# Paged decoding inside a hybrid decoder step: ScalarE's order at the softmax, and the rotated keys put last

## The chip, the core and the metric

One core of a Trainium2 chip runs the whole program. The metric is the device time of one execution in microseconds. Three executions of the kernel before gave 3480.07, 3480.68 and 3483.55 us.

## What is computed

The reference is one inference step of a trunk of two layers. Each layer projects its input once and feeds three groups of heads (a state-space mixer, latent attention, a gated delta rule); their outputs are joined, projected and normalised. It does this for a prompt of 1024 positions and for 8 sequences that decode 4 positions each. The change lies in the latent attention of these 8 sequences, which looks at 8192 cached positions per sequence:

```python
def attend(blk):
    ql, qr, qp = blk
    s = (jnp.einsum('bthr,bsr->bhts', ql, kv_lat)
         + jnp.einsum('bthd,bsd->bhts', qr, k_rope)).astype(jnp.float32) * MLA_SCALE
    s = jnp.where(k_pos[None, :] <= qp[:, None], s, -jnp.inf)
    p = jax.nn.softmax(s, axis=-1).astype(kv_lat.dtype)
    return jnp.einsum('bhts,bsr->bthr', p, kv_lat)
```

A cached position has a latent row of 256 numbers (`kv_lat`, which serves as key and as value) and a rotated key of 32 numbers (`k_rope`). With 8 heads and 4 new positions, each sequence has 32 queries. The cache is paged, so its rows are gathered by index.

## The kernel before, in words

Phase 2 of a layer (`phase2`, line 1422) holds the attention and the output projection. Two generators are woven into each other there by `weave_decode` (line 434): the decoding (`decode_units`, line 1691) and the attention of the prompt (`mla_prompt`, line 1488). The decoding yields a number, an amount of TensorE time; `weave_decode` then takes steps of the prompt's generator until they have paid that amount by the builder's clock, each step at 0.45 or more, and carries what is left over or overspent to the next yield. So the numbers in the yields say how much prompt work stands at which place of the decoding. Inside this weaving the order of the instructions of TensorE and of VectorE is the order of the program text; the orders of ScalarE, of GpSimd and of the DMA queues are planned by the framework's scheduler, which takes what is ready in its own plan, and of several ready instructions the one with the highest priority, by default the earliest in the text. `high_priority()` raises the priority of the instructions in its block. On the chip each engine follows its fixed order and waits for semaphores.

The decoding of a layer has 32 units, 8 sequences times 4 parts of 2048 positions. A unit does the following (names of tiles as the profile has them):

- `load` (line 1682) gathers the rows of a part with three indirect DMAs from GpSimd's queue (line 1680): two for latent rows into one of three buffers (dec_v<-cache_kv_latent), one for rotated keys into a ring of three (dec<-cache_k_rope). It is called at the end of a unit for the part three units on; the latents' buffer is free when the weighted values of this unit are done, the rotated keys' slot when VectorE has turned the keys in it.
- `turn` (line 1703, instruction at line 1704) turns half of the latent rows on VectorE in squares of 32, so that they can serve as keys (dec_k<-dec_v). Line 1773 (line 1759 for the first unit) does the same for the rotated keys (dec<-dec, into rT).
- `products` (line 1706) multiplies queries and keys on TensorE into the tile ps_dS: parts 0 to 3 are the first half of the latents' 256 numbers, 4 to 7 the second half, part 8 the rotated keys. Each part is 8 multiplications in tiles of 32 x 32, two records each in the profile, so 16 records a part and 144 a unit. There is one such tile.
- `softmax` (line 1714): VectorE takes the maximum over ps_dS (line 1717) and brings it into the form in which ScalarE needs it (lines 1720 to 1726); ScalarE takes the exponential and its sum (line 159, dec<-ps_dS,dec).
- `turned` (line 1734): TensorE turns the weights (ps_aT<-c,dec, 32 records), and ScalarE copies them out (line 1740, dec<-ps_aT).
- `weighted` (line 1743): TensorE multiplies weights and latent rows (ps_dV<-dec_v,dec, 32 records); `total` (line 1750) adds the result to the sequence's sum on VectorE (line 156, dec<-dec,dec,ps_dV).

The turning of the next unit's keys stands inside the unit: rotated keys and first half before `turned`, second half before `weighted`. After the third unit `decode_new` (line 1646) handles the new positions; its first step takes the bank of ps_dV.

The prompt's steps in between are products ps_aS, their maximum (line 1558, VectorE), the exponential (line 159, c<-ps_aS,c), a scaling of the weights by their sum (line 1575, ScalarE, after line 1571 on VectorE), the turning of the weights (ps_aT at line 150, copied out at line 1515 by ScalarE) and the weighted values ps_aO.

Line 180 is the helper that records every multiplication, line 150 every full transpose, lines 153, 156 and 159 those of VectorE, GpSimd and ScalarE.

Of the kernel before, what the change touches and what calls it, by code (L numbers as in the profile page):

```python
# [16 lines left out]
AF = mybir.ActivationFunctionType  # L17
# [7 lines left out]
SCALE = 96.0 ** -0.5  # L25
# [102 lines left out]
class Builder:  # L128
# [1562 lines left out]
    def decode_units(self, d):  # L1691

        nc, G, T, q5, q8, O = self.nc, d["G"], d["T"], d["q5"], d["q8"], d["O"]
        D = d["D"].rest()
        RP, RT, rT = Ring(D(1024)), Ring(D(1024)), D(512)
        rT4 = rT.rearrange("p (n c k) -> p n c k", n=8, c=2)
        H = [slice(0, 64), slice(64, 128)]  # L1700
        tmp = D(8)

        def turn(V, r):
            nc.vector.transpose(T[r].rearrange("p j s k -> p j (s k)"), V[:, :, r * 128:r * 128 + 128])  # L1704

        def products(b, sc, parts):
            for s in parts:
                for i, p in enumerate(G):
                    for c in range(2):
                        k = rT4[p, :, c] if s == 8 else T[s // 4].rearrange("p (n c) s k -> p n c s k", c=2)[p, :, c, s % 4]  # L1710
                        o = i % 2 * 512
                        self.mm(sc[G[i // 2 * 2 + c], o:o + 256], lhsT=q8[p, b] if s == 8 else q5[p, s, b], rhs=k, start=s == 8, stop=s == 7)

        def softmax(b, u, sc):
            s3 = sc.rearrange("p (i n) -> p i n", i=2)[:, :, 0:256]
            nm, al, m = d["m"][:, b, u:u + 1], d["al"][:, b, u:u + 1], tmp[:, 0:1]
            nc.vector.tensor_reduce(out=al, in_=s3, axis=AX.XY, op=ALU.max)  # L1717
            pe = RP(512)

            nc.vector.tensor_copy(out=m[H[0]], in_=al[H[1]])  # L1720
            nc.vector.tensor_scalar(out=m[H[0]], in0=m[H[0]], scalar1=al[H[0]], scalar2=-SCALE, op0=ALU.max, op1=ALU.mult)
            if u:
                old = d["m"][:, b, u - 1:u]
                self.tt(nc.vector, m[H[0]], m[H[0]], old[H[0]], ALU.min)
            for h in H:
                nc.vector.tensor_copy(out=nm[h], in_=m[H[0]])

            self.act(pe.rearrange("p (n i k) -> p i n k", n=8, i=2), s3.rearrange("p i (n k) -> p i n k", n=8), AF.Exp,
                     scale=SCALE, bias=nm, accum_out=d["sm"][:, b, u:u + 1])
            if u:  # L1730
                self.act(al, old, AF.Exp, scale=-1.0, bias=nm)
            return pe

        def turned(pe):
            ps, pt = self.psum("aT"), RT(512)
            for n in range(8):
                w = slice(n * 64, n * 64 + 64)
                for h in H:
                    self.mm(ps[h, w], lhsT=pe[h, w], rhs=self.ident[h, h], start=True, stop=True)
            nc.scalar.copy(out=pt, in_=ps)  # L1740
            return pt

        def weighted(V, pt):
            pv = self.psum("dV")
            for n in range(8):
                for c in range(2):
                    self.mm(pv[G[n % 2 * 2 + c], :256], lhsT=pt[:, n * 64 + c * 32:n * 64 + c * 32 + 32], rhs=V[:, 2 * n + c], start=n < 2, stop=n > 5)
            return pv

        def total(b, u, pv):  # L1750
            if u == 0:
                nc.vector.tensor_copy(out=O[:, b], in_=pv[:, :256])
            else:
                self.stt(O[:, b], O[:, b], d["al"][:, b, u:u + 1], pv[:, :256], ALU.mult, ALU.add)

        units = [(b, u) for b in range(DB) for u in range(4)]
        load, ready = d["load"], d["ready"]
        V, rr = ready.pop(0)
        nc.vector.transpose(rT, rr)
        turn(V, 0)  # L1760
        turn(V, 1)
        for k, (b, u) in enumerate(units):
            sc = d["ps"].tile([128, 1024], F32, name="ps_dS", tag="dS", bufs=1)
            products(b, sc, (8, 0, 1, 2, 3))
            yield 0.3
            products(b, sc, (4, 5, 6, 7))
            pe = softmax(b, u, sc)
            more = k + 1 < len(units)
            if more:
                Vn, rr = ready.pop(0)  # L1770
            yield 2.0
            if more:
                nc.vector.transpose(rT, rr)  # L1773
                turn(Vn, 0)
            pt = turned(pe)
            yield 0.8
            if more:
                turn(Vn, 1)
            pv = weighted(V, pt)
            if more:  # L1780
                V = Vn
            total(b, u, pv)
            if k + 3 < len(units):
                ready.append(load(*units[k + 3]))
            if k == 2:
                yield from self.decode_new(d)
            if k in (29, 30):
                next(d["projection"])
# [241 lines left out]
```

## Time and profile before

| | |
|---|---|
| median of three executions | 3480.68 us |
| the profiled execution | 3483.24 us |
| its span, first to last instruction | 3481.4 us |
| TensorE busy in the span | 3091.7 us, 89% |
| VectorE busy | 2216.9 us, 64% |
| ScalarE busy | 1325.7 us, 38% |
| GpSimd busy | 1176.1 us, 34% |
| mean granted clock of TensorE | 0.951 |

PE is TensorE's multiplications, PEld its weight loads (both are issued by one sequencer), DVE is VectorE, ACT ScalarE, POOL GpSimd, SP the engine that issues most DMAs. In a row of a group stand the line, the engine, what is written and read, the form and the count; then busy time and mean duration in ns; then the idle time of the engine just before these instructions, with what ended most of it. In an answer in order of time each row begins with start and length in us, and the bracket at its end has the idle time of the engine before the row and the instruction that ended it. "issue" means that the profile shows nothing that was waited for. A granted clock of 1.00 is 2.4 GHz for TensorE, 0.50 is 1.2 GHz.

### The profile page before, as it was taken

The page shows a single profiled execution, that of the slowest core. Times are in us where ns is not written, and L with a number is a line of the kernel's source. Part 1 is how long each engine was busy: PE and PEld are TensorE (multiplying, and loading weights), DVE is VectorE, ACT ScalarE, POOL GpSimd, SP SyncE. Part 2 cuts the span into 40 slices and gives each one's busy share as a digit, 9 for nine tenths or more (in the row PEclk, how much of TensorE's full clock was granted, in tenths as well). Part 3 has the DMA queues.
Part 4 walks back from the last instruction along what each step waited for, and adds up shares of the span by engine and source line. Part 5 has one row for each costly group of instructions (what it writes and reads, how often), then busy time and mean ns, then how long its engine had stood idle before and what let it go on. Part 6 is the DMA issues. An engine that isn't in the chain of part 4 may idle for free. (4 is left out here: it accounts for less than half of the span.)

```text
span 3481.4 us, 82579 instructions
## 1 busy us (share of the span) xinstructions
PE 3091.7 (89%) x33880; PEld 2621.0 (75%) x33880; DVE 2216.9 (64%) x4610; ACT 1325.7 (38%) x3099; POOL 1176.1 (34%) x1250
## 2 busy tenths in 40 slices
PE   5899999898777888899988999989897788888997
PEld 4889998798664555569978999888886555555797
DVE  6767366577555666655687663756876456667456
ACT  4433333343222333354543332443332233334544
POOL 3444434755432212120143444455454212112100
PEclk7999999899888999999999999999998899999999
DMA  3332323556876655535434232255669656554354
GB/s 127 122 102 88 106 73 124 166 180 196 275 240 221 203 184 190 183 126 187 161 103 128 92 97 94 69 168 161 185 211 326 215 179 209 193 186 161 118 204 136
DMA packets 317070, 564.70 MB, mean 162 GB/s; under 512 B 51772, under 2 KB 218748, under 8 KB 299668
## 3 DMA queue, kind: packets, MB, share of 16 engines
q1 hardware_dynamic: 293140, 408.42, 37.1%
q0 software_dynamic: 23552, 151.01, 12.0%
q8 instruction: 266, 4.36, 0.5%
q14 instruction: 112, 0.92, 0.1%
HBM read 429.00 MB, written 130.30 MB: 161 GB/s over the span
## 5 line engine op out<-in xcount | busy, mean ns | idle before, releaser
L180 PE MATMUL ps_pj<-xh,w_r 128*128 128x384 f32 (+1 forms) x4416 | 1205.7, 340 | 65.3 <-DVE p_cv L156 29.4
L180 PEld LDWEIGHTS ps_pj<-xh,w_r 128*128 128x128 f32 x4416 | 809.7, 194 | 83.9 <-DVE p_cv L156 33.3
L180 PE MATMUL ps_pj<-xl,w_r 128*128 128x384 f32 (+1 forms) x2208 | 731.9, 331 | 5.5 <-POOL xl L153 5.4
L180 PEld LDWEIGHTS ps_pj<-xl,w_r 128*128 128x128 f32 x2208 | 429.0, 194 | 15.6 <-POOL xl L153 14.0
L156 DVE SCALAR_TENSOR_TENSOR p_cv<-p_cv,c 128x384 f32<-128x384 f32 (+1 forms) x432 | 359.5, 834 | 63.7 <-ACT p_cv L159 57.2
L180 PE MATMUL ps_dS<-dec_k,c 32*32 32x256 f32 x8192 | 332.1, 383 | 18.4 <-DVE dec_k L1704 2.1
L153 POOL TENSOR_TENSOR w_r<-w_raw,w_r 128x1024 fp32r<-128x1024 f32 (+1 forms) x98 | 235.1, 2400 | 242.8 <-ACT w_r L165 220.4
L180 PEld LDWEIGHTS ps_dS<-dec_k,c 32*32 32x32 f32 x8192 | 184.5, 106 | 144.6 <-issue 104.4
L1704 DVE STREAM_TRANSPOSE dec_k<-dec_v 128x2048 f32<-128x2048 f32 x128 | 291.0, 2281 | 0.0
L1680 POOL DMA_INDIRECT dec<-cache_k_rope,c x64 | 60.7, 949 | 523.7 <-DVE dec L1773 521.2
L159 ACT ACTIVATE c<-ps_aS,c 128x512 f32<-128x512 f32 (+3 forms) x192 | 111.2, 579 | 215.7 <-DVE c L1559 214.5
L159 ACT ACTIVATE p_cv<-p_cv 128x384 f32<-128x384 f32 x144 | 72.4, 503 | 302.7 <-DVE p_cv L156 302.2
L1680 POOL DMA_INDIRECT dec_v<-cache_kv_latent,c x128 | 120.3, 940 | 183.8 <-PE ps_dV L180 122.9
L180 PE MATMUL ps_b<-p_b 128*128 128x128 f32 (+7 forms) x1476 | 154.2, 285 | 10.5 <-DVE p_b L156 3.7
L180 PE MATMUL ps_dV<-dec_v,dec 128*32 128x256 f32 x2048 | 129.5, 395 | 37.5 <-ACT dec L1740 34.8
L180 PE MATMUL ps_aS<-mix,wo 128*128 128x384 f32 (+1 forms) x960 | 159.6, 322 | 1.4 <-DVE wo L153 1.4
L1558 DVE TENSOR_REDUCE c<-ps_aS 128x1 f32<-128x512 f32 (+3 forms) x192 | 105.3, 548 | 84.0 <-PE ps_aS L180 81.2
L1717 DVE TENSOR_REDUCE dec<-ps_dS 128x1 f32<-128x512 f32 x64 | 44.2, 691 | 179.6 <-PE ps_dS L180 179.5
L153 DVE TENSOR_TENSOR wo<-c,wo 128x1024 fp32r<-128x1024 f32 x92 | 115.4, 1254 | 67.0 <-ACT wo L165 66.6
L1515 ACT COPY c<-ps_aT 128x512 f32<-128x512 f32 (+3 forms) x192 | 89.9, 478 | 177.6 <-PE ps_aT L150 157.2
L180 PEld LDWEIGHTS ps_aS<-mix,wo 128*128 128x128 f32 x960 | 152.1, 188 | 3.6 <-DVE wo L153 2.3
L165 ACT CAST wo<-c 128x1024 fp32r<-128x1024 f32 x96 | 100.5, 1047 | 141.3 <-PE ps_aS L180 70.6
(348 smaller groups left out, 6007.3 us busy)
## 6 DMA issues: line engine op xcount, KB each, us to landing
c<-w_out SPq DMA_DIRECT2D x96, 512.0 KB
w_raw<-w_in SPq DMA_DIRECT2D x92, 512.0 KB
pd<-p_cv SPq DMA_DIRECT2D x164, 192.0 KB
p_b<-pd SPq DMA_DIRECT2D x66, 256.0 KB
c<-pd SPq DMA_DIRECT2D x64, 256.0 KB
q<-rowd SPq DMA_DIRECT2D x48, 256.0 KB
p_b<-rowd SPq DMA_DIRECT2D x48, 256.0 KB
pd<-p_cv SPq DMA_DIRECT2D x82, 144.0 KB
```

The source lines that it names most:

```text
L153: eng.tensor_tensor(out=out, in0=a, in1=b, op=op)
L156: self.nc.vector.scalar_tensor_tensor(out=out, in0=a, scalar=s, in1=b, op0=op0, op1=op1)
L159: self.nc.scalar.activation(out=out, in_=in_, func=func, **kw)
L165: self.nc.scalar.copy(out=hi, in_=src)
L180: return self.nc.tensor.matmul(out, lhsT=lhsT, rhs=rhs, start=start, stop=stop)
L1515: nc.scalar.copy(out=t[:, :w], in_=p[:, :w])
L1558: nc.vector.reduce_max(out=m, in_=ps[:, :w], axis=AX.X)
L1680: nc.gpsimd.indirect_dma_start(out=out, out_offset=None, in_=src, in_offset=bass.IndirectOffsetOnAxis(ap=idx[:, c:c + 1], axis=0))
L1704: nc.vector.transpose(T[r].rearrange("p j s k -> p j (s k)"), V[:, :, r * 128:r * 128 + 128])
L1717: nc.vector.tensor_reduce(out=al, in_=s3, axis=AX.XY, op=ALU.max)
```

## The change

It touches `decode_units` alone, in five places.

1. In `products` the accumulation now begins with part 0 and ends with part 8. The first call of a unit takes parts 0 to 3, the second 4 to 8; before, part 8 was the first of the first call.
2. The exponential of `softmax` stands in a `high_priority()` block.
3. So does the copy of the turned weights.
4. The turn of the next unit's rotated keys (line 1773) moves from before the first half's turn to behind the second half's turn. The same holds ahead of the loop (line 1759).
5. The yields of a unit are 0.3, 1.7 and 1.2 where they were 0.3, 2.0 and 0.8.

```diff
-  self.mm(..., rhs=k, start=s == 8, stop=s == 7)
+  self.mm(..., rhs=k, start=s == 0, stop=s == 8)
...
-            self.act(pe.rearrange("p (n i k) -> p i n k", n=8, i=2), s3.rearrange("p i (n k) -> p i n k", n=8), AF.Exp,
-                     scale=SCALE, bias=nm, accum_out=d["sm"][:, b, u:u + 1])
+            with self.tc.high_priority():
+                self.act(pe.rearrange("p (n i k) -> p i n k", n=8, i=2), s3.rearrange("p i (n k) -> p i n k", n=8), AF.Exp,
+                         scale=SCALE, bias=nm, accum_out=d["sm"][:, b, u:u + 1])
...
-            nc.scalar.copy(out=pt, in_=ps)
+            with self.tc.high_priority():
+                nc.scalar.copy(out=pt, in_=ps)
...
-        nc.vector.transpose(rT, rr)
         turn(V, 0)
         turn(V, 1)
+        nc.vector.transpose(rT, rr)
         for k, (b, u) in enumerate(units):
             sc = d["ps"].tile([128, 1024], F32, name="ps_dS", tag="dS", bufs=1)
-            products(b, sc, (8, 0, 1, 2, 3))
+            products(b, sc, (0, 1, 2, 3))
             yield 0.3
-            products(b, sc, (4, 5, 6, 7))
+            products(b, sc, (4, 5, 6, 7, 8))
             pe = softmax(b, u, sc)
             more = k + 1 < len(units)
             if more:
                 Vn, rr = ready.pop(0)
-            yield 2.0
+            yield 1.7
             if more:
-                nc.vector.transpose(rT, rr)
                 turn(Vn, 0)
             pt = turned(pe)
-            yield 0.8
+            yield 1.2
             if more:
                 turn(Vn, 1)
+                nc.vector.transpose(rT, rr)
             pv = weighted(V, pt)
```

## Rows read from the trace of the kernel before

**Rows 1.** The page's first line.

```profile
span 3481.4 us, 82579 instructions
```

**Rows 2.** Table of stretches: stretch, length, busy (count) of PE, PEld, DVE, ACT, POOL, clock, DMA.

```profile
1050.00:1512.00 462.00, 402.32 (x7549) 253.11 (x7549) 297.03 (x646) 167.58 (x455) 87.88 (x91) 0.96 0.55 187
...
1512.00:1560.00 48.00, 45.13 (x337) 31.32 (x330) 26.27 (x97) 30.50 (x70) 15.51 (x16) 0.96 0.47 146
```

**Rows 3.** Groups of instructions, whole run: weighted values, turned weights.

```profile
L180 PE MATMUL ps_dV<-dec_v,dec 128*32 128x256 f32 x2048 | 129.5, 395 | 37.5 <-ACT dec L1740 34.8 <-ACT c L159 1.3 <-ACT c L1575 0.6
...
L180 PE MATMUL ps_aT<-c,dec 64*64 64x64 f32 x2048 | 77.4, 228 | 24.2 <-ACT dec L159 13.8 <-ACT c L1515 10.4
```

**Rows 4.** Waits of the tile dec, whole run: releaser or waiter, us, times.

```profile
  DVE dec L1726: 160.1, 50
...
  POOL dec L1680: 521.2, 56
...
  PE ps_dV L180: 34.8, 35
  PE ps_aT L180: 13.8, 22
```

**Rows 5.** One unit in order of time, first layer, from turned weights to weighted values.

```profile
1286.39 1.15 PE L180 MATMUL ps_aT<-c,dec 64*64 64x64 f32 x32 [0.23 <-ACT dec L159]
...
1288.10 1.01 ACT L1575 ACTIVATE c<-c 128x384 f32<-128x384 f32 x2 [0.94 <-DVE c L1571]
...
1288.57 0.70 DVE L1773 STREAM_TRANSPOSE dec<-dec 128x512 f32<-128x512 f32 x1
...
1289.19 2.27 DVE L1704 STREAM_TRANSPOSE dec_k<-dec_v 128x2048 f32<-128x2048 f32 x1
...
1289.57 0.57 ACT L1740 COPY dec<-ps_aT 128x512 f32<-128x512 f32 x1
...
1290.19 3.02 PE L180 MATMUL ps_dV<-dec_v,dec 128*32 128x256 f32 x32 [1.81 <-ACT dec L1740]
```

**Rows 6.** Weighted values of three other units; stretch 1291:1292 in columns of rows 2.

```profile
1273.79 3.61 PE L180 MATMUL ps_dV<-dec_v,dec 128*32 128x256 f32 x32 [1.62 <-ACT dec L1740]
...
1488.16 1.93 PE L180 MATMUL ps_dV<-dec_v,dec 128*32 128x256 f32 x32 [0.56 <-ACT dec L1740]
...
2785.87 3.62 PE L180 MATMUL ps_dV<-dec_v,dec 128*32 128x256 f32 x32 [1.01 <-ACT dec L1740]
...
1291.00:1292.00 1.00, 1.00 (x16) 0.48 (x12) 0.96 (x4) 0.01 (x1) 0.00 (x0) 0.50 0.65 184
```

**Rows 7.** A unit with gathers: their launches, and TensorE's weight loads.

```profile
1258.28 0.95 POOL L1680 DMA_INDIRECT dec<-cache_k_rope,c  x1 [8.93 <-DVE dec L1773]
...
1261.01 0.18 PEld L180 LDWEIGHTS ps_dS<-dec,c 32*32 32x32 f32 x16 [0.41 <-DVE c L1571]
...
1261.39 0.93 POOL L1680 DMA_INDIRECT dec_v<-cache_kv_latent,c  x1 [2.16 <-PE ps_dV L180]
...
1262.68 0.18 PEld L180 LDWEIGHTS ps_dS<-dec_k,c 32*32 32x32 f32 x5 [0.57 <-issue]
...
1264.15 0.60 PEld L180 LDWEIGHTS ps_dS<-dec_k,c 32*32 32x32 f32 x22 [0.56 <-issue]
```

**Rows 8.** A late unit without gathers, its products.

```profile
1490.02 0.18 PEld L180 LDWEIGHTS ps_dS<-dec,c 32*32 32x32 f32 x16 [0.41 <-issue]
...
1490.27 1.66 PEld L180 LDWEIGHTS ps_dS<-dec_k,c 32*32 32x32 f32 x64
1490.48 3.83 PE L180 MATMUL ps_dS<-dec_k,c 32*32 32x256 f32 x128
...
1492.35 1.48 PEld L180 LDWEIGHTS ps_dS<-dec_k,c 32*32 32x32 f32 x64 [0.42 <-DVE dec_k L1704]
```

**Rows 9.** Waits from 1050 to 1512 us: us in total, times, longest.

```profile
PEld ps_dS L180 <- DVE dec_k L1704: 4.6, 8, 1.9
...
PE ps_dV L150 <- DVE dec L156: 2.9, 1, 2.9
```

More of the change, by code (lines that the diff above doesn't have):

```diff
@@ L1711, in products @@
                         o = i % 2 * 512
-                        self.mm(sc[G[i // 2 * 2 + c], o:o + 256], lhsT=q8[p, b] if s == 8 else q5[p, s, b], rhs=k, start=s == 8, stop=s == 7)
+                        self.mm(sc[G[i // 2 * 2 + c], o:o + 256], lhsT=q8[p, b] if s == 8 else q5[p, s, b], rhs=k, start=s == 0, stop=s == 8)
         def softmax(b, u, sc):
```

## The prediction

> **What bounds the kernel now.** I began with the page's totals [rows 1], then the table of stretches [rows 2], then the groups of instructions and the waits of the decoding's own tile [rows 3, 4], and last single units in order of time [rows 5 to 8]. The change touches only the decoding loop, which runs from 1050 to 1512 us in the first layer and again in the second, so about 930 of 3481.4 us. In the first of these stretches TensorE is busy for 402.32 of 462 us and VectorE for 297.03 [rows 2]: TensorE sets the pace, in the order written out for it, and what can be won are its holes.
>
> Two holes belong to the change. Before the weighted values (tile ps_dV) TensorE is idle for 37.5 us in the whole run, and 34.8 us of that, in 35 of 64 units, end with ScalarE's copy of the turned weights, line 1740 [rows 3, 4]. Before the turning of the weights (ps_aT<-c,dec) it waits for the exponential: 13.8 us, 22 times [rows 3, 4].
>
> Why the copy is late can be seen in one unit [rows 5]. The weights are turned by 1286.39 + 1.15 = 1287.54. ScalarE then stands idle for 0.94 us, because the next instruction in its order is a scaling of prompt weights (line 1575) that waits for VectorE; it does that, a prompt exponential, and only at 1289.57 the copy. TensorE has nothing left to do from 1290.19 - 1.81 = 1288.38. That idle time also lowers its clock: the microsecond from 1291 has a granted clock of 0.50, which is the 1.2 GHz level, and the 32 products of that unit take 3.02 us, where 1.93 us is what they take at 2.4 GHz [rows 5, 6].
>
> **The change, part by part.** The durations are those of the profiled execution, 3483.24 us, which stands 2.56 us above the median of 3480.68.
>
> *Copy first, and 0.4 more prompt work at it.* A copy issued at 1287.6 ends 0.57 us later, at about 1288.2, before TensorE runs out of prompt work even without the additional 0.4. So I take all of the 34.8 us away but 1 us, for units with no prompt step in that place: 33.8. With the idle time goes the low clock. Four units show it at their weighted values, three of them in the rows: 3.61, 3.02 and 3.62 us against 1.93, a mean loss of 1.49, times four 5.9 us [rows 5, 6]. Together 39.7 us. Bounds: 0, if the order on ScalarE stays, and 39.7.
>
> *What is late next.* The next unit's products need the first half of the new keys turned (line 1704). In the unit shown that ends at 1289.19 + 2.27 = 1291.46. Moving the turn of the rotated keys, 0.70 us at 1288.57, behind it brings this to 1290.76. With the copy early and the full clock TensorE would be there at 1288.4 + 1.93 = 1290.3. Of the 1.81 + 1.09 = 2.90 us to win, about 0.5 stays as a new wait, 18%. Applied to 39.7 that is 7.1; 32.6 is left. Without the move it would be 1.1 us, so this part of the edit pays only through the copy.
>
> *Exponential first.* Nothing to win in most units: in 50 of 64 ScalarE already stands idle until VectorE's line 1726 hands it the maximum [rows 4]. I count 0. Where it would overtake prompt work, that work moves by 0.7 us at most.
>
> *0.3 less prompt work before the turned weights.* TensorE reaches the turning earlier and waits longer for the same exponential: 22 waits now, so 22 x 0.3 = 6.6 us. Bounds 0 and, if all 62 units with a successor come to wait, 18.6; I take 6.6, since the other units show no wait.
>
> *Prompt work that the copy overtakes.* Each of the 35 scalings or exponentials behind a copy comes 0.575 us later, 20 us at most, 0 at least: TensorE needs them mostly after the weighted values (1.93 us) and the first products (1.9 us or more), which cover it. I take 5. If that cover is missing, the wait has only changed its name.
>
> *Rotated keys multiplied last.* The 144 records of one unit's products stay; only the accumulation's first and last part change places. But the second half of the keys (second turn) is now needed after 64 instead of 80 records: 128 records take 3.83 us with a wait of 0.42 in them [rows 8], so 16 take (3.83 - 0.42)/8 = 0.43, and the half is needed that much earlier. Such waits are 8 in the first layer, 4.6 us [rows 9], and 0.42 us where nothing else holds the products up [rows 8]. About seven more of 0.42 make 3 us; bounds 0 and 62 x 0.43 = 27. The turned rotated keys themselves end 0.70 us after the second turn and are needed 64 records (4 x 0.43 = 1.7 us) later: covered.
>
> *Turn of the rotated keys last on VectorE.* Behind it now stands the total (line 156). Only once per layer does anybody wait for that: the first step on the new keys, 2.9 us [rows 9]. It becomes 0.70 longer, 1.4 us in two layers.
>
> *GpSimd's queue.* The gather of the rotated keys waits for that turn, 56 times [rows 4]. Today it is launched before the weighted values (1258.28), the two gathers of latent rows after them (1261.39, the second right behind the first) [rows 7]. Afterwards the turn ends behind the second turn, so its launch comes right behind the latents' two, amid the products. What a launch there may cost is seen on TensorE: with the two latent gathers the weight loads of the first products last from 1261.01 to 1264.15 + 0.60, 3.74 us, with pauses of 0.57 us that wait for nothing; in a late unit with no gather they last from 1490.02 to 1490.27 + 1.66, 1.91 us [rows 7, 8]. So two launches cost 1.83 us, one 0.92. Bounds for the third: 0 (where it is launched today no pause follows) and 56 x 0.92 = 51 us. It will mostly come some time after the second launch, when TensorE has been fed again; I take 0.1 each, 6 us, nearer to the row of the same gather. That its data land later costs nothing: they are used three units on.
>
> *Prompt work in all.* 3.2 instead of 3.1 per unit, 6 us of steps in both layers that leave the stretch behind the loop, where TensorE is busy 45.13 of 48 us [rows 2]. Moved from one busy stretch to another: 0; if that stretch were bound by something else, up to 6 either way. SP's few loads and stores of these steps move with them.
>
> Sum: 32.6 - 6.6 - 5 - 3 - 1.4 - 6 = 10.6 us less. From 3483.24 that is 3472.6, and 2.56 lower, as the median stands to this execution, **3470 us**.
>
> **The rivals.** *The third launch stalls TensorE (slower).* The mechanism is the one just described: launch pauses hit the products, and the gather of rotated keys leaves a place where they are hidden. For it speaks that its launch takes as long as the latents' (0.95 against 0.93 us [rows 7]); against it that no pause is seen behind it today, though there TensorE stands idle or has work queued. At 0.6 us each, 34 us take the place of my 6, and the time is 3470 + 28 = 3498. It decides from (10.6 + 6)/56 = 0.3 us per launch. Chance 0.16. The Trainium skill, "DMA: Bandwidth & Descriptors", section "SWDGE vs HWDGE vs iDMA", states that for each DMA issued by GpSimd a program there writes descriptors into rings in SBUF; by this rule small rows would cost the same launch as large ones, and the third launch would stand at the upper bound, 51 us. Whether TensorE pays for it no row here shows for the rotated keys.
>
> *ScalarE's order hardly changes (the change doesn't do what it says).* A priority only decides between instructions that are ready at the same time in the scheduler's plan; a prompt scaling planned before the weights were turned stays ahead. Then only the additional prompt work helps: at most 35 x 0.4 = 14 us, less 18%, 11.5, against 6.6 + 3 + 1.4 + 6 = 17. That gives 3480.7 + 5.5 = 3486. For it speaks that the planned order let ScalarE idle in front of line 1575 at all. Chance 0.18.
>
> *The costs stay at their lower ends.* Then 32.6 - 1.4 = 31 us are won: 3450. Chance 0.14: each cost was put near its lower end already.
>
> **How the numbers follow.** My forecast has 0.52, with a range of its own from 3458 to 3482. About 0.2%, 7 us, is what a measurement of this kernel can tell from no change. Of the 0.52 some 0.38 is faster by more, 0.12 within, 0.02 slower; of the unchanged order 0.03, 0.09 and 0.06; the low costs are faster (0.14), the third launch slower (0.16). Faster 0.55, same 0.21, slower 0.24. The range from 3450 to 3498 leaves out half of each outer case, and little of the rest.
>
> **What would show it.** Right: the idle time before ps_dV put down to line 1740 falls from 34.8 to a few us; line 1740 starts within 0.1 us of the turned weights' end; no low clock at the weighted values; waits of ps_dS for line 1704 grow by some us. Wrong: the copies still stand behind line 1575; idle time before ps_aT grows by more than 10 us; or the weight loads of the products show a fourth and fifth pause, behind a gather of rotated keys that is launched after the latents'.

## The result: 1.65% slower, and the profile after

The changed kernel took 3538.55 us (median of four executions, 3535.04 to 3549.26), the kernel before 3482.11 us beside it: a ratio of 1.0165, 95% interval 1.0139 to 1.0191. The forecast was 3470 us and its range ended at 3498. The execution profiled here, the slowest of the four, took 3549.26 us and has a span of 3547.5 us, 66 us more than that of before [rows 1].

The page's first line and the table of stretches, in the columns of rows 2 (the first layer's decoding now ends some 30 us later, so the second stretch still decodes):

```profile
span 3547.5 us, 82542 instructions
...
1050.00:1512.00 462.00, 407.42 (x6997) 245.64 (x7003) 278.85 (x610) 161.89 (x434) 80.78 (x86) 0.93 0.52 177
1512.00:1560.00 48.00, 40.57 (x721) 28.20 (x706) 33.98 (x113) 23.41 (x56) 10.76 (x9) 0.96 0.43 138
```

In the same 462 us TensorE is busy a little longer than before (407.42 against 402.32 [rows 2]) and yet does less: 6997 records in place of 7549. A part of that is the clock, 0.93 in place of 0.96.

The waits of the tile dec (waiter, us, times), whole run:

```profile
  POOL dec_v L1680: 544.3, 48
...
  POOL dec L1680: 196.5, 48
...
  PE ps_aT L180: 29.6, 38
  PE ps_dV L180: 11.5, 14
```

The weighted values wait 11.5 us for the copy where they waited 34.8 [rows 4], so 23.3 us were won there. The turned weights wait 29.6 us for the exponential where they waited 13.8: 15.8 us lost. In GpSimd's queue the long wait has changed its place: it stood before the rotated keys' gather (521.2 us [rows 4]) and now stands before the latents' gathers (544.3 us). In most units all three launches now fall amid the products that follow the weighted values.

The groups of the decoding's multiplications, after:

```profile
L180 PE MATMUL ps_dS<-dec_k,c 32*32 32x256 f32 x8192 | 382.1, 411 | 71.3 <-issue 49.7 <-DVE dec_k L1704 2.0
L180 PEld LDWEIGHTS ps_dS<-dec_k,c 32*32 32x32 f32 x8192 | 182.4, 112 | 245.6 <-issue 200.3 <-DVE c L1559 5.8 <-DVE dec_k L1704 4.1
L180 PEld LDWEIGHTS ps_dS<-dec,c 32*32 32x32 f32 x1024 | 32.8, 117 | 14.1 <-issue 9.7
L180 PE MATMUL ps_dV<-dec_v,dec 128*32 128x256 f32 x2048 | 124.8, 384 | 11.9 <-ACT dec L1742 11.5
L180 PE MATMUL ps_aT<-c,dec 64*64 64x64 f32 x2048 | 79.1, 231 | 44.2 <-ACT dec L159 29.6 <-ACT c L1515 14.2
L180 PE MATMUL ps_dS<-dec,c 32*32 32x256 f32 x1024 | 61.4, 415 | 3.6 <-issue 3.1
```

And the products of before, which rows 3 did not show:

```profile
L180 PE MATMUL ps_dS<-dec_k,c 32*32 32x256 f32 x8192 | 332.1, 383 | 18.4 <-DVE dec_k L1704 2.1 <-issue 0.4
L180 PEld LDWEIGHTS ps_dS<-dec_k,c 32*32 32x32 f32 x8192 | 184.5, 106 | 144.6 <-issue 104.4 <-DVE dec_k L1704 5.8 <-DVE c L1570 0.2
L180 PEld LDWEIGHTS ps_dS<-dec,c 32*32 32x32 f32 x1024 | 11.8, 106 | 61.5 <-issue 48.5 <-DVE dec_k L1704 3.7 <-DVE c L1571 2.5
...
L180 PE MATMUL ps_dS<-dec,c 32*32 32x256 f32 x1024 | 44.8, 408 | 34.9 <-issue 34.9
```

Busy and idle time added up, the products took 332.1 + 18.4 + 44.8 + 34.9 = 430.2 us before and 382.1 + 71.3 + 61.4 + 3.6 = 518.4 after: 88.2 us more. The weighted values won (129.5 + 37.5) - (124.8 + 11.9) = 30.3 us [rows 3], the turning of the weights lost (79.1 + 44.2) - (77.4 + 24.2) = 21.7. So the products alone are more than the whole loss. The word that stands behind their weight loads' idle time is "issue", a wait for nothing that the profile shows: 200.3 + 9.7 = 210.0 us in place of 104.4 + 48.5 = 152.9, 57 us more. (The two rows have to be added, since the idle time before a layer's first product, 39 us in the two layers together after and 35 before, stands in the row of the part that is multiplied first.)

What it is can be seen in one unit, GpSimd's launches and TensorE's weight loads in order of time:

```profile
1156.33 1.05 PEld L180 LDWEIGHTS ps_dS<-dec_k,c 32*32 32x32 f32 x47 [0.41 <-DVE c L1573]
1156.70 0.94 POOL L1680 DMA_INDIRECT dec_v<-cache_kv_latent,c  x1 [11.04 <-PE ps_dV L180]
1157.94 0.94 POOL L1680 DMA_INDIRECT dec_v<-cache_kv_latent,c  x1 [0.30 <-issue]
1158.00 0.16 PEld L180 LDWEIGHTS ps_dS<-dec_k,c 32*32 32x32 f32 x4 [0.62 <-issue]
...
1159.19 0.95 POOL L1680 DMA_INDIRECT dec<-cache_k_rope,c  x1 [0.30 <-issue]
...
1160.27 0.10 PEld L180 LDWEIGHTS ps_dS<-dec_k,c 32*32 32x32 f32 x1 [0.58 <-issue]
1160.97 1.67 PEld L180 LDWEIGHTS ps_dS<-dec_k,c 32*32 32x32 f32 x67 [0.60 <-issue]
```

Two launches brought three pauses of about 0.57 us (rows 7 show two of them). With the third launch right behind them there are five (at 1158.00, 1158.76, 1159.52, 1160.27 and 1160.97), between which TensorE loads only a few weights. The launches' timing within one trace tells the launch from the late turn. In 42 units of this run the two latent gathers are launched at 0.38 and 1.62 us after the first product. In the 20 of them in which the third launch comes by 3.06 us, right behind, the pauses (of 0.5 us and more) add up to 2.81 us a unit; in the 22 in which it comes between 3.27 and 4.1 us they are 2.08 us, and in 13 of these only the old three pauses are left. In two units more, one late in each layer, there is no third launch: three pauses each, 1.77 us. The rotated keys are turned late in all 44. One of the 22:

```profile
1214.31 1.12 PEld L180 LDWEIGHTS ps_dS<-dec_k,c 32*32 32x32 f32 x46 [0.41 <-issue]
1216.00 0.16 PEld L180 LDWEIGHTS ps_dS<-dec_k,c 32*32 32x32 f32 x5 [0.58 <-issue]
...
1217.51 0.17 PEld L180 LDWEIGHTS ps_dS<-dec_k,c 32*32 32x32 f32 x7 [0.60 <-issue]
...
1218.08 0.95 POOL L1680 DMA_INDIRECT dec<-cache_k_rope,c  x1 [1.23 <-DVE dec L1780]
...
1218.69 1.47 PEld L180 LDWEIGHTS ps_dS<-dec_k,c 32*32 32x32 f32 x64 [0.17 <-issue]
```

The pauses are not the whole price. In 14 of the 20 units TensorE's clock falls to its 1.2 GHz level in the same unit, behind the pauses; in the 22 it does so twice. One of the 14, with its weight loads behind the last pause and then two stretches in the columns of rows 2 (compare the 1.47 us for 64 loads above):

```profile
1176.23 2.84 PEld L180 LDWEIGHTS ps_dS<-dec_k,c 32*32 32x32 f32 x63 [0.60 <-issue]
...
1171.00:1175.00 4.00, 3.51 (x71) 1.32 (x63) 3.54 (x5) 1.08 (x3) 2.38 (x3) 1.00 0.50 149
1175.00:1180.00 5.00, 4.78 (x89) 3.82 (x85) 0.00 (x0) 0.00 (x0) 0.44 (x1) 0.66 0.96 370
```

In the decoding of both layers together the clock stands at 1.2 GHz for 143 us, in the kernel before for 68.

### The profile page after: what moved, and what is told of

It reads as the page before. It is cut to its first block, busy times and chain, and to the rows that moved or that the text cites. A ratio compares the mean times of both kernels' runs of the same rounds, so it can differ in the third digit from the quotient of the medians.

```text
span 3547.5 us, 82542 instructions
## 1 busy us (share of the span) xinstructions
PE 3151.6 (89%) x33880; PEld 2639.6 (74%) x33880; DVE 2218.6 (63%) x4610; ACT 1331.6 (38%) x3099; POOL 1177.4 (33%) x1250
## 5 line engine op out<-in xcount | busy, mean ns | idle before, releaser
L180 PE MATMUL ps_dS<-dec_k,c 32*32 32x256 f32 x8192 | 382.1, 411 | 71.3 <-issue 49.7
L180 PEld LDWEIGHTS ps_dS<-dec_k,c 32*32 32x32 f32 x8192 | 182.4, 112 | 245.6 <-issue 200.3
L1680 POOL DMA_INDIRECT dec_v<-cache_kv_latent,c x128 | 120.5, 941 | 583.5 <-PE ps_dV L180 544.3
L1717 DVE TENSOR_REDUCE dec<-ps_dS 128x1 f32<-128x512 f32 x64 | 44.2, 691 | 255.0 <-PE ps_dS L180 255.0
L180 PEld LDWEIGHTS ps_b<-p_b 128*128 128x128 f32 (+5 forms) x1476 | 131.3, 161 | 27.2 <-issue 11.9
L1558 DVE TENSOR_REDUCE c<-ps_aS 128x1 f32<-128x512 f32 (+3 forms) x192 | 105.1, 548 | 71.3 <-PE ps_aS L180 68.3
L165 ACT CAST w_r<-w_raw 128x1024 fp32r<-128x1024 f32 (+1 forms) x98 | 100.2, 1022 | 129.5 <-PE ps_pj L180 113.2
```

Source lines behind the costliest of these rows:

```text
L165: self.nc.scalar.copy(out=hi, in_=src)
L180: return self.nc.tensor.matmul(out, lhsT=lhsT, rhs=rhs, start=start, stop=stop)
L1558: nc.vector.reduce_max(out=m, in_=ps[:, :w], axis=AX.X)
L1680: nc.gpsimd.indirect_dma_start(out=out, out_offset=None, in_=src, in_offset=bass.IndirectOffsetOnAxis(ap=idx[:, c:c + 1], axis=0))
```

## The experiments

Eighteen runs, in seven groups; the runs of a group share a chip and the executions of the kernel before.

### One part of the change at a time

**Turn back.** The changed kernel with

```diff
+                nc.vector.transpose(rT, rr)
                 turn(Vn, 0)
...
                 turn(Vn, 1)
-                nc.vector.transpose(rT, rr)
```

and the same ahead of the loop.

> The changed kernel with one part undone: the rotated keys are turned before the first half's turn again, as in the kernel before (the order of the products, the priorities and the yields stay as changed). In the planned order of GpSimd's queue the gather of rotated keys then stands ahead of the two latent gathers again. Theory A (the third launch amid the products pauses TensorE; the profile of the changed kernel has 55 us more pauses that wait for nothing before the products' weight loads, and 72 us more at the lower clock): the products have three pauses per unit again, and the time falls by 55 to 75 us, to 3465 to 3485 us. Theory B (0.3 less prompt work before the turned weights: waits for the exponential grew by 22 us, and the idle time lowers the clock): the time stays at 3515 us or more. If both hold, it is between.

Measured: 3477.67 us, ratio to before 0.9973 (0.9963 to 0.9984). Each of the 56 units with two launches amid its products has three pauses again, and the clock is back: 55 us at 1.2 GHz in the decoding of both layers. The first layer's:

```profile
1055.00:1514.00 459.00, 403.11 (x7580) 252.02 (x7575) 297.52 (x655) 176.18 (x466) 87.52 (x90) 0.97 0.56 188
```

**Turn alone.** The kernel before with the edits 1 and 4 of the change (rotated keys multiplied last, turned last).

> The kernel before with two parts of the change alone: rotated keys multiplied last and turned last; no priorities, yields as before. Theory A: the pauses come with this part, there is none of the gain at the copy (27 us less idle time in the changed kernel), so the time is 3530 to 3565 us. Theory B: 3475 to 3495 us, since the yields are what they were.

Measured: 3566.86 us, 1.0235 (1.0222 to 1.0248). That is 2 us beyond what theory A gave. The pauses between 0.5 and 5 us among the products' weight loads, with no releaser, are 217, 143 us in all; in the kernel before 168 and 97 us, in the changed one 208 and 134 us, with the turn put back 168 and 100 us. The decoding has 138 us at 1.2 GHz.

**Priorities alone.** The kernel before with edits 2 and 3.

> The kernel before with the two high priorities alone. Theory of the prediction (the copy comes first in ScalarE's order through the priority): 3440 to 3465 us. Rival (a priority decides only between instructions that are ready together in the plan): the planned order of each of the five engines is the same, instruction for instruction, as that of the kernel before, so the time is the same within 0.2%, 3475 to 3489 us, and the idle time before the weighted values put down to the copy stays at 34.8 us within a few us.

Measured: 3488.21 us, 1.0001 (0.9990 to 1.0011). The row that should have moved:

```profile
  PE ps_dV L180: 32.5, 33
```

**Yields alone.** The kernel before with edit 5.

> The kernel before with the yields alone (0.3, 1.7, 1.2). Theory A: the gain at the copy comes from this part (idle time before the weighted values falls from 34.8 us to about 12) and so does the loss at the exponential (13.8 to some 30 us); together 3470 to 3488 us. Theory B (less prompt work before the turned weights is what made the change slower): 3515 us or more.

Measured: 3473.63 us, 0.9968 (0.9957 to 0.9980). The same waits:

```profile
  PE ps_aT L180: 29.8, 40
...
  PE ps_dV L180: 15.9, 17
```

What follows: theory B falls. The yields alone bring the gain at the copy (34.8 to 15.9 us) and the loss at the exponential (13.8 to 29.8), and are 0.3% faster in sum. The priorities do nothing: the instructions of all five engines stand in the order of before, one for one. The turn that goes last, with what it does to GpSimd's queue, makes the kernel slower by 2.35%.

### Launches taken away or moved, and a second level of time

**Rotated keys' gathers left out.** The changed kernel with

```diff
-            gather(rr, rop, b * 12 + 8 + u)
+            if b * 4 + u < 3:
+                gather(rr, rop, b * 12 + 8 + u)
```

> The changed kernel without the gathers of rotated keys after the third part of each layer: it leaves out those 58 launches and their data (the later parts take the first three parts' rotated keys) and turns and multiplies as before, so the turn still stands last. Theory A (the launch is what costs): three pauses per unit at the products, as with the turn put back, and 3455 to 3490 us. Rival A2 (not the launch but the late turn of the rotated keys on VectorE is what holds the products up): 3515 us or more.

**Late loads.** A unit's loads are called one unit later, behind the softmax. A read of the old rows by VectorE holds the gathers back until then:

```diff
             pe = softmax(b, u, sc)
+            if k and k + 2 < len(units):
+                nc.vector.tensor_copy(out=tmp[:, 1:2], in_=Vp[:, 0, 0:1])
+                ready.append(load(*units[k + 2]))
...
-            if k + 3 < len(units):
-                ready.append(load(*units[k + 3]))
```

(Vp is the buffer of the unit before.) This in the changed kernel, in the kernel before, and in the kernel before with the new yields:

> The changed kernel with the loads moved: a unit's loads are called one unit later, behind the softmax's maximum, and a read of one element of the old latent rows by VectorE stands there, so that the two latent gathers can be launched only when the products are done, amid prompt work; the data have one unit less to arrive. Theory A (a launch pauses TensorE where it issues many small instructions, as in the products, and costs nothing amid prompt work of few large ones): the pauses at the products go, five per unit in the changed kernel, and the time falls by 100 to 170 us, to 3370 to 3440 us. Rival A3 (a launch pauses TensorE wherever it falls): the pauses move with the launches to the prompt's instructions and the time stays within 30 us of 3540. Rival A4 (the rows then arrive too late): VectorE's turn waits for the gather, and the time is longer.

> The kernel before with the loads moved in the same way. Theory A: the three pauses per unit at the products (99 us in all) go; if nothing takes their place 3380 to 3420 us. Rivals A3 and A4: 3470 us or more.

> The kernel before with the yields of the change and the loads moved in the same way: both gains together if they are independent, 10 us below the same without the new yields, 3370 to 3410 us.

Measured: 0.9967 (0.9953 to 0.9981) without the gathers; 1.0037 (1.0024 to 1.0050), 1.0051 (1.0034 to 1.0069) and 1.0044 (1.0028 to 1.0060) with late loads. But the kernel before took 3394.05 us in this group (3389.92 to 3405.62, 20 executions) and not 3486.32 (3478.66 to 3494.54, 24 executions) as in the group above, and nearly no pauses stand in the products even where the latent gathers are launched as before. So the times expected in us do not apply, and these runs could not show what moving a launch does to a pause. Against a kernel without pauses late loads only cost. The next group was made to read this level itself.

**Both kernels again.** The kernel before, the changed kernel, late loads with the new yields, gathers left out.

> The kernel before itself, for its trace on the chip of these runs. In the runs with late loads and with the rotated keys' gathers left out, the kernel before took 3394 us beside them, 92 us less than beside the four runs with one part each, and none of the four showed the pauses at the products, even where the latent gathers are launched at the same place as before. Theory C (the pauses behind a launch are a trait of the chip or of the placement, not of the program): at 3480 to 3490 us its trace shows some 170 pauses of 99 us in all, at 3390 to 3400 us nearly none; no time between.

> The changed kernel itself. Theory C: where the kernel before takes 3480 to 3490 us, some 220 pauses and a ratio of 1.012 to 1.020; where it takes 3390 to 3400 us, no pauses, and a ratio of 0.994 to 1.000, as with the rotated keys' gathers left out. Rival (the late turn slows the kernel by itself, on any chip): 1.012 to 1.020 in both cases.

> The yields of the change and the loads moved behind the softmax's maximum, again. Theory C with A: where the kernel before takes 3480 to 3490 us, the products have no pauses though the kernel before has them on this chip, and the ratio is 0.975 to 0.985 (92 us of pauses less, 13 us of new waits and reads more, as measured against 3394 us); where it takes 3390 to 3400 us, 1.004 again. Rival A3 (the pauses follow the launches to the prompt's work): 0.995 or more in the first case.

> The changed kernel without the gathers of rotated keys after the third part of each layer, again (it leaves out these launches and their data; the turn stays last). Theory A with C: ratio 0.995 to 0.999 on either kind of chip, with some 170 pauses where the kernel before has them. Rival A2 (the late turn is what costs): 1.010 or more where the kernel before takes 3480 to 3490 us.

Measured: the kernel before 3394.97 us (29 executions beside the four), and as a run of its own 1.0013 (0.9999 to 1.0026). The changed kernel 3386.00 us, **0.9978** (0.9963 to 0.9994): faster here. Late loads 1.0067 (1.0049 to 1.0085) where 1.004 was expected, without the gathers 0.9973 (0.9959 to 0.9987). Page and groups of the kernel before on this chip, then those of the changed kernel:

```profile
span 3389.6 us, 82579 instructions
...
L180 PE MATMUL ps_dS<-dec_k,c 32*32 32x256 f32 x8192 | 251.8, 382 | 12.9 <-DVE dec_k L1704 12.7
...
L180 PE MATMUL ps_dS<-dec,c 32*32 32x256 f32 x1024 | 44.2, 402 | 35.9 <-issue 35.9
```

```profile
span 3379.1 us, 82542 instructions
...
L180 PE MATMUL ps_dS<-dec_k,c 32*32 32x256 f32 x8192 | 254.7, 383 | 55.7 <-issue 38.5 <-DVE dec_k L1704 17.3
...
L180 PE MATMUL ps_dS<-dec,c 32*32 32x256 f32 x1024 | 41.3, 374 | 0.0
```

The same 82579 instructions as in rows 1 take 91.8 us less. The products are 251.8 + 12.9 + 44.2 + 35.9 = 344.8 us, so of the 430.2 us that they take in the profile of before 85.4 are the pauses and what hangs on them. In the changed kernel they are 351.7 us, 6.9 more, where it was 88.2 more on the other chip. Of the pauses, counted as above, one is left in the trace of either kernel. The unit from above, in the changed kernel on this chip: three launches at the same distances, no pause.

```profile
1139.78 1.49 PEld L180 LDWEIGHTS ps_dS<-dec_k,c 32*32 32x32 f32 x64 [0.41 <-DVE c L1573]
1140.16 0.94 POOL L1680 DMA_INDIRECT dec_v<-cache_kv_latent,c  x1 [8.83 <-PE ps_dV L180]
1141.40 0.94 POOL L1680 DMA_INDIRECT dec_v<-cache_kv_latent,c  x1 [0.30 <-issue]
1141.65 1.48 PEld L180 LDWEIGHTS ps_dS<-dec_k,c 32*32 32x32 f32 x64 [0.37 <-DVE dec_k L1704]
1142.64 0.95 POOL L1680 DMA_INDIRECT dec<-cache_k_rope,c  x1 [0.30 <-DVE dec L156]
```

What follows: theory C holds. There are two kinds of chips (or of whatever else goes with the chip that a group of runs gets). On the first kind the kernel before takes 3482 to 3489 us and launches stop TensorE; on the second it takes 3393 to 3397 us and they don't. No time between was seen in eight comparisons, four of each kind. On the second kind the changed kernel, with its late turn, is 0.2 to 0.4% faster, with or without the launches; the turn by itself was not run there.

### The launch on a chip of the first kind

**Launch moved alone**, the gathers left out and the late loads once more. The first is the kernel before with

```diff
                 turn(Vn, 1)
+                nc.vector.tensor_copy(out=tmp[:, 2:3], in_=rr[:, 0:1])
```

> The kernel before with one instruction more per unit: behind the second half's turn VectorE reads one element of the rotated keys that it has turned long before, so that the gather into their slot can be launched only then, behind the latents' gathers and amid the products, though the turn itself stays first and is multiplied first. Theory A with C: where the kernel before takes 3480 to 3490 us, the launch alone brings the loss: 1.012 to 1.025, with 200 pauses or more; where it takes 3390 to 3400 us, 0.998 to 1.004, with none. Rival A2 (the late turn is what costs, not the launch): 0.998 to 1.005 on either kind of chip.

> The changed kernel without the gathers of rotated keys after the third part of each layer (it leaves out these launches and their data; the turn stays last), for a chip on which the kernel before takes 3480 to 3490 us. There theory A gives three pauses per unit and a ratio of 0.990 to 1.000, the rival A2 1.010 or more. On the other kind of chip 0.997 again.

> The yields of the change and the loads moved behind the softmax's maximum, for a chip on which the kernel before takes 3480 to 3490 us. There theory A gives a ratio of 0.975 to 0.985 with nearly no pauses at the products, the rival A3 (the pauses follow the launches to the prompt's work) 0.995 or more. On the other kind of chip 1.004 to 1.007 again.

Measured, again on a chip of the second kind (before 3397.36 us): 0.9995 (0.9984 to 1.0005), 0.9962 (0.9949 to 0.9975) and 1.0053 (1.0038 to 1.0069). All three agree with what was expected for that kind; for the first kind these runs say nothing.

**Late loads, on the first kind.**

> The yields of the change and the loads moved behind the softmax's maximum, once more for a chip on which the kernel before takes 3480 to 3490 us. There theory A gives a ratio of 0.975 to 0.985 with nearly no pauses at the products; the rival A3 (the pauses follow the launches to the prompt's work) 0.995 or more. On the other kind of chip 1.004 to 1.007 again.

Measured: 3511.67 us, before 3485.22, ratio 1.0074 (1.0056 to 1.0093). A miss, and the most instructive one. The regular pauses at the products are gone (16 left, 12 us in all; the same kernel has 14 on the second kind), and the kernel is slower all the same. The launches now fall amid prompt work, and here is what stands still there; first the copy's group, then one unit in order of time:

```profile
L1740 ACT COPY dec<-ps_aT 128x512 f32<-128x512 f32 x64 | 37.3, 582 | 106.1 <-remote 68.7 <-PE ps_aS L180 17.1 <-PE ps_aT L150 16.4
```

```profile
1233.93 0.94 POOL L1680 DMA_INDIRECT dec_v<-cache_kv_latent,c  x1 [10.89 <-PE ps_aO L180]
...
1234.31 0.75 PE L180 MATMUL ps_aT<-c,dec 64*64 64x64 f32 x20
...
1235.17 0.94 POOL L1680 DMA_INDIRECT dec_v<-cache_kv_latent,c  x1 [0.30 <-issue]
...
1236.42 0.95 POOL L1680 DMA_INDIRECT dec<-cache_k_rope,c  x1 [0.31 <-issue]
...
1238.36 0.58 ACT L1740 COPY dec<-ps_aT 128x512 f32<-128x512 f32 x1 [2.57 <-remote]
1238.46 0.56 DVE L1558 TENSOR_REDUCE c<-ps_aS 128x1 f32<-128x384 f32 x1 [0.63 <-remote]
```

The weights are turned by 1235.06. The copy that waits for them starts at 1238.36, and VectorE's maximum, which waits for other products of TensorE, 0.10 us after it: both 1.0 us after the third launch has ended (1236.42 + 0.95). ScalarE stands idle before it from 1235.79, VectorE from 1237.83; "remote" is a releaser that the profile finds in no engine's row. So what the launches stop is not only TensorE's next weight load; what TensorE has finished by the trace (whose ends of multiplications are modelled) is not taken up by its readers either, until they are over. The trace also has the times at which TensorE's semaphore was raised: five times between 1238.34 and 1238.50, 0.03 to 0.06 us apart, for multiplications that end between 1235.06 and 1236.22. The decoding has 30 such bursts of three and more, each 0.8 to 1.6 us behind the end of a launch; the same kernel on a chip of the second kind has none there, and none of the copy's 68.7 us of "remote" time. Behind these waits the clock falls too: 141 us at 1.2 GHz in the decoding, 58 on the second kind. The rival that the delay follows the launches was right.

**Launches drawn apart.** The kernel before with the new yields; the second half's gather is called behind the next unit's softmax, and VectorE writes one element of its buffer there first, so that it can't be launched earlier:

```diff
+            if k and k + 2 < len(units):
+                nc.vector.memset(self.second[0][:, 2048:2049], 0.0)
+                self.second[1]()
```

So the first half's gather comes behind the weighted values, amid the products, as before; the second half's about 7 us later; the rotated keys' after their turn, as before.

> The yields of the change and the three launches of a unit drawn apart: the first half's gather stays behind the weighted values, amid the products; the second half's waits until VectorE has written one element of its buffer behind the softmax's maximum; the rotated keys' follows their turn, before the weighted values. On a chip on which the kernel before takes 3480 to 3490 us, theory S (only launches right behind one another hold the other engines up; the single one before the weighted values shows no pause there) gives nearly no pauses at the products and 0.968 to 0.978. Theory U (each launch costs its share wherever it falls amid the products, 0.9 us) gives one or two pauses per unit, 65 to 115 in all, and 0.978 to 0.990. Theory V (the delay follows every launch to whatever then hands over work) gives new waits of ScalarE or VectorE and 0.990 or more. On a chip without pauses: 0.996 to 1.003.

> The three launches of a unit drawn apart, with the yields of the change, once more for a chip on which the kernel before takes 3480 to 3490 us. There theory S (only launches right behind one another hold the others up) gives nearly no pauses at the products and 0.968 to 0.978; theory U (each launch amid the products costs its share, 0.9 us) one or two pauses per unit, 65 to 115 in all, and 0.978 to 0.990; theory V (the delay follows every launch) new waits of ScalarE or VectorE and 0.990 or more. On a chip without pauses: 0.998 to 1.001 again.

Measured on the second kind (before 3393.37 us) 0.9993 (0.9979 to 1.0006), and on the first kind, on the chip of the one-part runs, 3414.20 us beside 3488.53: **0.9792** (0.9774 to 0.9809). The products' weight loads, and one unit:

```profile
L180 PEld LDWEIGHTS ps_dS<-dec_k,c 32*32 32x32 f32 x8192 | 176.2, 106 | 95.4 <-issue 41.2 <-DVE dec_k L1708 14.1 <-DVE dec L1756 0.3
```

```profile
1180.85 0.94 POOL L1680 DMA_INDIRECT dec_v<-cache_kv_latent,c  x1 [1.77 <-PE ps_dV L180]
...
1182.12 1.00 PEld L180 LDWEIGHTS ps_dS<-dec_k,c 32*32 32x32 f32 x34 [0.59 <-issue]
...
1188.22 0.94 POOL L1680 DMA_INDIRECT dec_v<-cache_kv_latent,c  x1 [6.44 <-DVE dec_v L1773]
```

A launch by itself amid the products costs one pause (55 in the run, 33 us in all), two right behind one another cost three, three up to five. Theory U had the pauses a little too high (65 to 115) and theory S had none; the time lies where U begins. This version is faster than both kernels on the first kind of chip, and as fast as the kernel before on the second.

## Why the prediction was wrong

**The step that failed** is "GpSimd's queue": "I take 0.1 each, 6 us, nearer to the row of the same gather". Turning the rotated keys last costs the difference between the changed kernel and the one with the turn put back, 1.0165 - 0.9973 = 0.0192, or 67 us (worked out from two groups of runs, both of the first kind), 1.2 us for each of 56 launches; by itself (turn alone) 82 us, 1.5 us each. That is eleven times what I took, and beyond the bound of 51 us, which I had drawn in proportion from two launches. The price has two parts. The pauses are 208 in place of 168 with the turn put back, 34.5 us more or 0.6 us a launch: the size that the rival had given them (34 us). The rest is the clock, for which neither the step nor its rival had a term, although "Copy first" had read off how idle time lowers it: 143 us of the decoding at 1.2 GHz in place of 55, an estimated 44 us lost if all of it was bound by TensorE, half of the 88 us more. Behind the three pauses of two launches the clock hardly falls (less than 2 us over the 56 units with the turn put back), behind four and five it often does, so two launches could not price the third in proportion. The row that I leaned on, a rotated keys' launch with no pause behind it, showed a launch that stood alone ahead of 32 records; it could not price one that comes right behind two others. The rival that names this mechanism, and the sign in the trace by which it would show (a fourth and a fifth pause), were right; its time of 3498 us, without the clock, was too low, and so, as it came out, was its chance of 0.16.

The Trainium skill, "DMA: Bandwidth & Descriptors", section "SWDGE vs HWDGE vs iDMA", states that a program on GpSimd writes the descriptors of a DMA issued there. By that rule the small rows would be as dear to launch as the large ones; the traces agree as to the launch itself (means of 949 and 941 ns in the changed kernel), and what it does to the other engines only the first kind of chip shows.

**Copy first.** The mechanism was wrong, and the rival of the unchanged order right in it: a priority decides between what is ready together in the plan, and here it decided nothing (1.0001). In the changed kernel 25 of the 64 copies still come right behind line 1575, as many as before, which was one of the signs of being wrong. Of the 33.8 us of idle time foreseen 23.3 went all the same; the yields alone, with 0.4 more prompt work at the copy, take 18.9 away, where that rival had expected 11.5 at most. Of the 5.9 us for the low clock at the weighted values 129.5 - 124.8 = 4.7 came.

**0.3 less prompt work before the turned weights.** Right mechanism, wrong size: 15.8 us of waiting for the exponential where I took 6.6, since 16 more units came to wait (38 in place of 22); the upper bound of 18.6 was nearer. The two steps together, the yields alone, are -0.32%, 11 us.

**What is late next, products' order, turn last on VectorE.** Foreseen 7.1, 3 and 1.4 us. With the products' order changed and the turn put back the ratio is 0.9973, with the yields alone 0.9968: no difference to be seen. On the second kind of chip, where launches bring no pauses, the whole change gains 7.6 us (0.9978), where the sum without the 6 us for GpSimd was 16.6 and with it 10.6.

So the sum has the right sign on a chip on which a launch is free, but that is in part luck: the gain at the copy came through the yields and not through the priority, and the wait for the exponential took back 9.2 us more than foreseen. The profile that I read was from a chip on which a launch is not free, and the pauses in rows 7 were the warning.

**Open.** What makes the two kinds of chip differ; one chip came twice, both times of the first kind, so it may be the chip, but the runs can't exclude what else goes with it. By what way a launch holds up TensorE's weight loads and the raising of its semaphore. How much of the 67 us is the clock: the 44 us are an estimate, and no run changes the clock alone. And the launch moved alone has no run on the first kind, so that it, and not the late turn, costs the 67 us there rests on the units of one trace (2.81 against 2.08 and 1.77 us), on the second kind's 0.9995 and 0.9978, and on the pauses and waits following the launches in the two runs that moved them on the first kind.

## What to carry to other kernels

Count the launches of one queue that come right behind one another, not only how many there are, and look at what runs beside them: where a profile has pauses that wait for nothing, price the next launch in their midst by them, and add what a lower clock would cost behind them: here that was, by an estimate, about as much again. Draw launches apart by giving each a reader or writer of its own to wait for; that was worth 1.8% here on the kind of chip that shows the pauses (0.9792 against 0.9968 with the yields alone, on the same chip), and moving the burst as a whole made the kernel slower. And before counting on a priority, see whether the planned order of the engine changes at all.

## What was not expected of the hardware

The same program, instruction for instruction, takes 3394.97 us on one chip and 3486.32 us on another, both medians of 24 and more executions, and by a profile of each kind 85 us of the difference stand in the products. And a launch on GpSimd, 0.94 us of its own time, can hold back work that three other engines do: TensorE's weight loads by 0.59 us each time, and behind three launches, a copy on ScalarE and a maximum on VectorE until 1.0 us after the last has ended, when TensorE's semaphore is raised several times in a row for work that the trace has as ended up to 3.3 us before. Behind four or five pauses in a unit TensorE's clock often fell to 1.2 GHz (14 of the 20 units), and what that cost is an estimate of the same size as the pauses themselves.
